# Tokens of a block ordered by column first, and attention's interior steps over 368 keys instead of 384

## The chip, the cores and the metric

The kernel runs on one core of one Trainium2 chip. Five engines work side by side there, each on its own queue of instructions: TensorE (PE; its weight loads are listed as PEld), VectorE (DVE), ScalarE (ACT), GpSimd (POOL) and SyncE (SP), which here issues nearly all transfers. Matmuls write to PSUM, a memory of eight banks of 128 x 512 fp32; everything else works in SBUF. The metric is the device time of one execution in microseconds; lower is better.

## The reference

One encoder layer over 1024 tokens that form a grid of 16 rows x 64 columns, with 1024 channels:

```python
u = rms_norm(x, g1); proj = u @ w_in            # q k v cB cC cH gA gB
q, k = rms_norm(q), rms_norm(k)                 # per head, 8 heads of 64
y_a = neighbourhood_attention(q, k, v, rpb) @ w_attn_branch
y_b = (cB * conv3(cC * cH)) @ w_conv_branch     # width 3 along the tokens
x = x + (sigmoid(gA) * y_a + sigmoid(gB) * y_b) @ w_o
x = x + square(relu(rms_norm(x, g2) @ w_mlp_in)) @ w_mlp_out
```

In the attention each token sees a window of 8 rows x 16 columns. The window is clamped inside the grid, and a learned bias by relative row and column is added to the scores before the softmax. The convolution runs over the tokens in their natural order, row after row.

## The kernel before

**Blocks.** The host cuts the grid into 8 blocks of 16 rows x 8 columns, so a block has 128 tokens, one for each partition of a tile. Within a block, token (r, c) stands at place 8r + c: rows first, and 8 neighbouring columns beside each other. All activations are kept in this block order. Only the convolution needs the natural order, because its taps are the token ahead and the token behind.

**Precision.** An fp32 value is kept as two fp16 halves, high and low, and a product takes three passes (`PASSES`: high x high, high x low, low x high).

**Attention** (lines 946 to 1033) runs in 64 steps: 4 pairs of heads `p`, 8 blocks `i` of queries, 2 heads `e` of the pair. A query block looks at the keys of its own block and of the two beside it. That makes 3 x 128 = 384 keys for the interior blocks 1 to 6 (48 steps) and 256 for the edge blocks 0 and 7 (16 steps). The stages of one step are spread over about 15 rounds of the loop at line 1044:

- `at_qk` (L959): two matmuls, for the two halves of q, into a PSUM bank of the tag "s", of which there are three.
- `at_max` (L973): one VectorE operation adds bias and mask to the negated scores, writes them to `sz` (five buffers), and takes the minimum, which frees the PSUM bank.
- `at_exp` (L982, ScalarE), `at_recip` (L986, L987, VectorE, once for a pair), `at_hi` (L995, ScalarE) and `at_lo` (L999, VectorE) give the probabilities as two fp16 halves in `P16`. One `P16` tile holds both heads of a pair, and three of them take turns.
- `at_turn` (L1004): SyncE issues one DMA transpose for a pair, `P16` to `PT`.
- `at_pv` (L1016): for every key block, pass and head one matmul with 64 columns of v as weights, 18 for an interior pair of steps. They are issued for four pairs together, in every eighth round.
- `at_out` (L1029, L1032): the result goes back into the place of q.

**Convolution.** The same rounds carry the matmuls of the gated convolution. `emit` (L1039) puts 7 to 9 of its matmuls behind each QK, from the generator `conv_mms`. For each of four channel groups j there are three projections g, two halves of 512 tokens each, 24 matmuls for a half. They use the three PSUM banks of the tag "d". `conv_post` takes a finished bank: for g = 0, ScalarE copies it into `z` (L847); for g = 1, VectorE multiplies it into `z` (L852); for g = 2, VectorE multiplies the convolved `cv` by it (L861). `z` and `cv` are in natural order (row, block, column), and the view `perm` walks them in block order. Between them, `conv_taps` makes the three taps (L868 ScalarE, L872 VectorE, L875 and L878 GpSimd). `conv_split` then scales the result and writes it to `BT` in two halves: L897 on ScalarE copies the high half, L902 on GpSimd subtracts for the low half. `BT` is read later by the matmuls of branch B.

**Order.** The order on each engine is the order in which the program issues the work: it is written out by hand in the loop at line 1044. Weights for later matmuls are prepared in the same rounds: `fill` advances generators of chunks (L266, L297, L306) as long as a running count of VectorE time, `debt`, stays under a bound. Tiles of the pool `p2` are opened when the tiles of the q/k stage are closed, and take over their memory; a first write to such memory waits for the last reader of what was there.

**Constants.** The bias of a query block against three key blocks comes from the host as `rel`, 128 x 768 for a pair of heads, and the masks as `masks`. Both are laid out in the order of the tokens within a block.

Of the kernel before, what the change touches and what calls it, by code (L numbers as in the profile page):

```python
# [11 lines left out]
F16 = mybir.dt.float16  # L12
BF16 = mybir.dt.bfloat16
I32 = mybir.dt.int32
AF = mybir.ActivationFunctionType
# [3 lines left out]
D = 1024  # L19
S = 1024  # L20
H = 8
HD = 64
# [30 lines left out]
def encoder_block(ctx: ExitStack, tc: tile.TileContext, x, weights, cols, gqk, rel, masks, out):  # L53
    nc = tc.nc
    V, A, G, T, SP = nc.vector, nc.scalar, nc.gpsimd, nc.tensor, nc.sync
# [10 lines left out]
    def bank(tag):  # L66
        return psum.tile([128, 512], F32, name="ps_" + tag, tag=tag, bufs=banks[tag])
# [80 lines left out]
    def spend(v=0, a=0):  # L148

        debt[0] += v  # L150
        debt[1] += a
# [44 lines left out]
    def ones_col():  # L196
        turn[0] = (turn[0] + 1) % 4
        return ones[:, 128 + turn[0]:129 + turn[0]]
# [192 lines left out]
    VT = base.tile([128, 8, 2, 512], F16, name="vT", tag="V")  # L391
# [207 lines left out]
    c = ones_col()  # L599
# [40 lines left out]
    c = ones_col()  # L640
# [128 lines left out]
    for n, (kind, b) in enumerate(todo):  # L769
# [3 lines left out]
        ps = bank("do"[n % 2])  # L773
# [5 lines left out]
        if n == 3:  # L779
# [52 lines left out]
    w2p = p2.enter_context(tc.tile_pool(name="p2", bufs=2, reuse_waits="tile"))  # L832

    def perm(t, half=None):
        v = t.rearrange("p (r b c) -> p b r c", r=16, b=8)
        return v if half is None else v[:, 4 * half:4 * half + 4]

    def conv_post(j, g, half, ps, d):

        ch = cConv[j]  # L840
        p3 = ps.rearrange("p (b r c) -> p b r c", b=4, r=16)
        if g == 0:
            if half == 0:
                d["z"] = w2p.tile([128, S + 2], F32, name="z", bufs=1)
                G.memset(d["z"][:, 0:1], 0.0)
                G.memset(d["z"][:, S + 1:S + 2], 0.0)
            A.activation(perm(d["z"][:, 1:S + 1], half), p3, AF.Copy, scale=sc[:, ch.inv])  # L847
            spend(0, 600)
            return
        if g == 1:  # L850
            zn = perm(d["z"][:, 1:S + 1], half)
            V.tensor_tensor(zn, p3, zn, op=OP.mult)  # L852
            spend(620)
            if half == 1:
                d["cv"] = w2p.tile([128, S], F32, name="cv", bufs=1)
                conv_tail.append(conv_taps(ch, d))
            return
        while not d.get("taps"):
            yield
        cv = d["cv"]  # L860
        V.tensor_tensor(perm(cv, half), p3, perm(cv, half), op=OP.mult)  # L861
        spend(620)
        if half == 1:
            conv_tail.append(conv_split(j, cv))

    def conv_taps(ch, d):
        z, cv, c = d["z"], d["cv"], ch.cwj
        A.activation(cv, z[:, 0:S], AF.Copy, scale=sc[:, at(c, 0)])  # L868
        spend(0, 1020)
        yield  # L870
        yield
        V.scalar_tensor_tensor(cv, z[:, 1:S + 1], sc[:, at(c, 1)], cv, op0=OP.mult, op1=OP.add)  # L872
        spend(1200)
        yield
        G.tensor_scalar(z[:, 2:], z[:, 2:], sc[:, at(c, 2)], 1.0, op0=OP.mult, op1=OP.mult)  # L875
        yield
        for c in range(0, S, 256):
            G.tensor_tensor(cv[:, c:c + 256], cv[:, c:c + 256], z[:, c + 2:c + 258], op=OP.add)  # L878
        yield
        yield  # L880
        d["taps"] = True

    def conv_split(j, cv):
        ch = cConv[j]
        m, s, inv = tmp(), tmp(), tmp()
        A.activation(BT[:, 1, j].bitcast(BF16), cv, AF.Square, accum_out=sc[:, m])
        spend(0, 1150)
        yield
        V.tensor_scalar(sc[:, m], sc[:, m], 1e-36, None, op0=OP.max)
        yield  # L890
        yield from pow2_half(m, 14, s, inv)
        mul(inv, ch.inv, at(rowsB, j))
        G.tensor_scalar(cv, cv, sc[:, s], 1.0, op0=OP.mult, op1=OP.mult)
        yield
        yield
        bh, bl = (BT[:, w, j].rearrange("p (b r c) -> p b r c", b=8, r=16) for w in range(2))
        A.activation(bh, perm(cv), AF.Copy)  # L897
        spend(0, 1020)
        yield
        pv = perm(cv)  # L900
        for b in range(0, 8, 2):
            G.tensor_tensor(bl[:, b:b + 2], pv[:, b:b + 2], bh[:, b:b + 2], op=OP.subtract)  # L902

# [41 lines left out]

    steps = [(p, i, e) for p in range(4) for i in range(8) for e in range(2)]
    N = len(steps)
    st, obank = {}, {}

    def rng(i):  # L950
# [3 lines left out]
    def at_qk(s):  # L954
        p, i, e = steps[s]
        lo, nb = rng(i)
        ps = bank("s")
        for w in range(2):
            T.matmul(ps[:, :nb * 128], QD[:, p, e, w, i * 128:(i + 1) * 128],  # L959
                     KD[:, 2 * p + e, lo * 128:(lo + nb) * 128], start=w == 0, stop=w == 1)  # L960
        st[s] = {"ps": ps, "n": nb * 128}

    def at_max(s):
        p, i, e = steps[s]
        d = st[s]
        t, m = bias[p]
        if 0 < i < 7:
            bm = m[:, e]
        else:
            bm = (t[:, e, 1:3] if i == 0 else t[:, e, 0:2]).rearrange("p b k -> p (b k)")  # L970
        z = d["z"] = w2p.tile([128, 384], F32, name="sz", bufs=5)
        d["mx"] = tmp()
        V.tensor_tensor_reduce(z[:, :d["n"]], d["ps"][:, :d["n"]], bm, sc[:, cneg], 3.0e38, OP.add, OP.min,  # L973
                               accum_out=sc[:, d["mx"]])
# [14 lines left out]

    def at_hi(s):  # L990
        d = st[s]
        n, e = d["n"], s % 2
        P = d["P"] = w2p.tile([128, 1536], F16, name="P16", bufs=3) if e == 0 else st[s - 1]["P"]
        d["hi"], d["lo"] = (P[:, (2 * e + w) * n:(2 * e + w + 1) * n] for w in range(2))
        A.activation(d["hi"], d["z"][:, :n], AF.Copy, scale=sc[:, d["r"]])  # L995

    def at_lo(s):
# [3 lines left out]
    def at_turn(s):  # L1001
        d = st[s]
        PT = d["PT"] = w2p.tile([128, 12, 128], F16, name="PT", bufs=6)
        SP.dma_start_transpose(PT[:, :4 * d["n"] // 128], d["P"][:, :4 * d["n"]])  # L1004

    def at_pv(s):
        p, i, _ = steps[s]
        lo, nb = rng(i)
        if i % 4 == 0:
            obank[p, i // 4] = bank("o")  # L1010
        O = obank[p, i // 4]
        seq = [(k, sp, sv) for k in range(nb) for sp, sv in PASSES]
        for n, (k, sp, sv) in enumerate(seq):
            for e in range(2):
                hd = (2 * p + e) * HD
                T.matmul(O[64 * e:64 * e + 64, (i % 4) * 128:(i % 4 + 1) * 128],  # L1016
                         VT[:, lo + k, sv, hd:hd + HD], st[s]["PT"][:, (2 * e + sp) * nb + k],
                         start=n == 0, stop=n == len(seq) - 1)
        for e in range(2):
            del st[s + e]  # L1020
# [20 lines left out]
    debt[:] = [0, 0]  # L1041
    for k in range(N + 16):
        p, w = k // 16, k % 16
        if p < 3 and w == 3:
            bias[p + 1] = bias_load(p + 1)
        if p < 3 and w in (12, 14):
            bias_make(*bias[p + 1], (w - 12) // 2)
            spend(550)
        ok = lambda d: 0 <= k - d < N
        debt[:] = [max(0, v - SPAN) for v in debt]  # L1050
# [44 lines left out]
    p3 = ExitStack()  # L1095
# [74 lines left out]

    def forms_split(ch, t, s, P):

# [91 lines left out]
    for n in range(8):  # L1264
# [3 lines left out]
        m = w3p.tile([128, 2, 512], F32, name="m", bufs=1)  # L1268
# [315 lines left out]
    y = []  # L1584
# [265 lines left out]
    for n in range(28):  # L1850
        s, o = n // 7, n % 7
        need(16 + n)
        P = OPS.pop(16 + n)
        inv = c2[s].inv
        for j in range(4):
            bk = anybank()
            for c, m in ((0, 256), (256, 256)) if n == 27 and j == 3 else ((0, 512),):
                ps = bk[:, c:c + m]
# [29 lines left out]

def _masks():

    r = np.arange(16)[:, None, None, None, None]
    c = np.arange(8)[None, :, None, None, None]
    bb = np.arange(3)[None, None, :, None, None]
    kr = np.arange(16)[None, None, None, :, None]
    kc = np.arange(8)[None, None, None, None, :]
    start = np.clip(r - 4, 0, 8)
    row = (kr >= start) & (kr < start + 8)
    rel = 8 * bb + kc - c
    colm = (rel >= 0) & (rel <= 15)
    full = (16, 8, 3, 16, 8)  # L1900
    row, colm = (np.broadcast_to(a, full).reshape(128, 384) for a in (row, colm))
    return np.stack([np.where(a, 0.0, NEG) for a in (row, colm)], 1).astype(mybir.dt.np(mybir.dt.bfloat16))

# [40 lines left out]
```

## Time and profile before

| | |
|---|---|
| time, median of 3 runs | 1207.05 us (1206.65 to 1208.08) |
| profiled execution, first to last instruction (its span) | 1205.3 us |
| granted TensorE clock, mean | 1.000 |
| QK matmuls, first and last start | 153.9 to 288.5 us |
| PV matmuls, first and last start | 187.6 to 304.8 us |

The profile shows one execution. The span leaves out what lies before its first and behind its last instruction, so it is a little shorter than a measured time. The page gives each engine's busy time, then the chain of waits that ended last. Its groups have the line, the engine, the operation, the tiles written and read, the shape and the count, then the busy time, the mean time of one instruction in ns, and the idle time of the engine just before them with what ended it. A view of one line gives minimum, median and maximum in ns with the first and last start. The timeline gives the start, the length, and in brackets the idle time ahead. An idle engine costs something only where TensorE, or whatever sets the end, waits for it.

### The profile page before, as it was taken

The numbers are of one execution on the slowest core, as the hardware profiler recorded it, in microseconds if no ns is written. First come the engines' busy times: TensorE is split into PE (matmuls) and PEld (weight loads), VectorE is DVE, ScalarE is ACT, GpSimd is POOL, SyncE is SP. The second block draws the span as 40 slices with busy tenths as digits, with TensorE's granted clock in tenths as the row PEclk, the third lists the DMA queues.
The fourth block names the chain that finished last, engine by engine and source line by source line (L and its number), as shares of the span: only waits on it lengthen the run. The fifth ranks groups of instructions, "written<-read, shape, count | busy, mean of one in ns | idle before, by whom it ended". The sixth has DMA issues, their size and how long they took to land.

```text
span 1205.3 us, 17076 instructions
## 1 busy us (share of the span) xinstructions
PE 1188.0 (99%) x6294; PEld 573.8 (48%) x6294; DVE 938.7 (78%) x1759; ACT 759.8 (63%) x1183; POOL 433.1 (36%) x280
## 2 busy tenths in 40 slices
PE   6999999999999999999999999999999999999998
PEld 4444445555444444444467444444444444444444
DVE  7777988988368787877878655545548999999997
ACT  7766679867554545337779778678676744746440
POOL 1640011222311112001004465565567471553662
PEclk9999999999999999999999999999999999999999
DMA  7766657676542211224386545445465925334202
GB/s 264 151 213 141 140 119 130 133 146 123 103 123 65 67 56 53 70 93 187 57 155 183 182 159 192 149 139 193 145 247 201 352 97 217 129 138 194 105 35 105
DMA packets 171012, 173.36 MB, mean 144 GB/s; under 512 B 131504, under 2 KB 132016, under 8 KB 166832
## 3 DMA queue, kind: packets, MB, share of 16 engines
q1 hardware_dynamic: 170352, 168.07, 47.9%
q10 hardware_dynamic: 576, 4.19, 0.8%
q8 instruction: 49, 0.80, 0.3%
q14 instruction: 35, 0.29, 0.1%
HBM read 102.51 MB, written 37.75 MB: 116 GB/s over the span
## 4 chain that ended last, share of the span: by engine, by line
PE 73%; DVE 9%; ACT 1%; issue 1%; DMA 1%; DVEq 0%; ACTq 0%
PE ps_d L210 26%; PE ps_s L210 23%; PE ps_o L210 16%; PE ps_d L1039 6%; DVE w_s L1163 2%; PE ps_o L1016 1%; PE ps_s L959 1%; DVE sg L1279 1%; DVE P L999 1%; DMA u2T<-v 1%; DVE sz L973 1%; ACT w_s L1167 0%; DVE sc L317 0%; DVE m L1281 0%; ACT sg L1245 0%
## 5 line engine op out<-in xcount | busy, mean ns | idle before, releaser
L210 PEld LDWEIGHTS <-ops 128*128 128x128 f16 x1356 | 132.4, 98 | 157.3
L210 PEld LDWEIGHTS <-w 128*128 128x128 f16 x1368 | 132.8, 98 | 140.0 <-DMA u2T<-v 0.6
L1039 PE MATMUL ps_d<-uT,w_ws 128*128 128x512 f16 x528 | 123.7, 379 | 0.1
L210 PE MATMUL ps_d<-ops 128*128 128x512 f16 (+1 forms) x528 | 118.3, 374 | 0.0
L1765 ACT ACTIVATE ops<-hf,sc 128x2048 f16<-128x2048 f32 x26 | 52.0, 2000 | 97.9 <-PE ps_o L210 35.2
L210 PE MATMUL ps_s<-ops 128*128 128x512 f16 x492 | 112.9, 379 | 0.0
L1152 POOL TENSOR_TENSOR tsum<-raw 128x512 f32<-128x512 f32 x28 | 46.0, 1658 | 149.6 <-ACT raw L1138 141.6
L1345 POOL TENSOR_TENSOR as<-as 128x512 f32<-128x512 f32 x56 | 77.5, 1384 | 39.3 <-ACT as L1625 36.0
L210 PEld LDWEIGHTS <-w_s 128*128 128x128 f16 x588 | 56.8, 98 | 69.4 <-DVE w_s L1163 1.9
L210 PE MATMUL ps_d<-u2x,w 128*128 128x512 f16 (+1 forms) x360 | 80.0, 372 | 0.0
L210 PEld LDWEIGHTS <-uT 128*128 128x128 f16 x504 | 49.0, 98 | 59.6 <-DMA uT<-u 0.8
L1039 PEld LDWEIGHTS <-w_ws 128*128 128x128 f16 x528 | 51.2, 98 | 54.5 <-DVE cv L861 0.4
L210 PE MATMUL ps_o<-ops 128*128 128x512 f16 x336 | 77.1, 379 | 0.0
L1767 DVE SCALAR_TENSOR_TENSOR ops<-hf,sc,ops 128x2048 f16<-128x2048 f32 x26 | 74.0, 2846 | 3.7 <-ACT ops L1765 3.7
L210 PE MATMUL ps_o<-u2T,w 128*128 128x512 f16 (+1 forms) x324 | 71.7, 371 | 0.0
L1138 ACT ACTIVATE raw<-raw,sc 128x256 f32<-128x256 f32 x172 | 71.0, 493 | 0.8 <-DMA raw<-in_weights 0.7
L1152 POOL TENSOR_TENSOR gsum<-raw 128x512 f32<-128x512 f32 x14 | 19.0, 1376 | 133.0 <-issue 72.8
L1167 ACT ACTIVATE w<-raw,sc 128x512 f16<-128x512 f32 (+1 forms) x28 | 24.6, 927 | 54.1 <-DVE sc L426 54.1
L297 DVE SCALAR_TENSOR_TENSOR w_ws<-raw,sc,w_ws 128x512 f16<-128x512 f32 (+2 forms) x72 | 51.2, 763 | 4.7 <-ACT w_ws L306 4.7
L1658 DVE TENSOR_TENSOR as<-ps_d,as 128x512 f32<-128x512 f32 (+1 forms) x14 | 9.4, 672 | 55.8 <-ACT as L1677 53.4
L210 PE MATMUL ps_s<-u2T,w 128*128 128x512 f16 (+1 forms) x252 | 52.7, 359 | 0.0
L982 ACT ACTIVATE sz<-sz,sc 128x384 f32<-128x384 f32 (+1 forms) x64 | 37.2, 582 | 22.5 <-DVE sc L973 15.0
(357 smaller groups left out, 2629.5 us busy)
## 6 DMA issues: line engine op xcount, KB each, us to landing
raw<-in_weights SPq DMA_DIRECT2D x88, 512.0 KB, 5.4
hs<-as SPq DMA_DIRECT2D x16, 1792.0 KB, 8.7
hf<-hs SPq DMA_DIRECT2D x26, 1024.0 KB, 6.3
w2x<-in_weights SPq DMA_DIRECT2D x16, 512.0 KB, 8.1
raw<-in_weights SPq DMA_DIRECT2D x16, 384.0 KB, 3.5
xt<-in_x SPq DMA_DIRECT2D x8, 512.0 KB, 10.0
gs<-s ACTq DMA_DIRECT2D x4, 1024.0 KB, 4.0
x<-in_x SPq DMA_DIRECT2D x8, 512.0 KB, 9.8
```

The lines of the kernel that those rows point to most:

```text
L210: T.matmul(ps, l, r, start=a, stop=b)
L297: V.scalar_tensor_tensor(lo, self.raw[p][:, o:o + m], sc[:, c:c + 1], hi, op0=OP.mult, op1=OP.subtract)
L959: T.matmul(ps[:, :nb * 128], QD[:, p, e, w, i * 128:(i + 1) * 128], KD[:, 2 * p + e, lo * 128:(lo + nb) * 128], start=w == 0, stop=w == 1)
L982: A.activation(z, z, AF.Exp, scale=-1.0, bias=sc[:, d["mx"]], accum_out=sc[:, d["sm"]])
L1039: T.matmul(ps, l, r, start=a, stop=b)
L1138: A.activation(v, v, AF.Copy, scale=sc[:, at(g, 4 * i + k)])
L1152: G.tensor_tensor(t[:, o], a, b, op=OP.add)
L1163: V.scalar_tensor_tensor(o(1), w, sc[:, s], o(0), op0=OP.mult, op1=OP.subtract)
L1167: A.activation(o(0), w, AF.Copy, scale=sc[:, s])
L1345: sub.tensor_tensor(z[o], z[a], z[b], op=op)
L1765: A.activation(P[:, 1, 0], hf, AF.Copy, scale=sc[:, Rs])
L1767: V.scalar_tensor_tensor(P[:, 1, 1], hf, sc[:, Rs], P[:, 1, 0], op0=OP.mult, op1=OP.subtract)
```

## The change

Within a block, token (r, c) now stands at place 16c + r: columns first, and the 16 rows of a column beside each other. A query in column c of its block needs, of the 24 columns of three key blocks, those from c to c + 15, so at most the columns 0 to 22. In the new order the unneeded column 23 is the last 16 of the 384 keys. The interior steps therefore compute scores, maximum, exponential and halves over 368 keys. In `P16` each part keeps its room of 384 with the last 16 columns set to zero once, by three memsets on GpSimd ahead of the loop; the transpose moves all of it as before, and for the third key block the PV matmuls contract over 112 rows. Three named tiles take the place of the rotating `P16`. The evacuations of the convolution read a PSUM bank whose 128 tokens of a block are now (column, row), walking it in the order of `z` and `cv`; L897 writes `BT` in the new order, and the four subtractions at L902 walk `cv` by rows. The host lays out input, output, bias and masks in the new order, outside the measured time.

```diff
     def conv_post(j, g, half, ps, d):
-        p3 = ps.rearrange("p (b r c) -> p b r c", b=4, r=16)
+        p3 = ps.rearrange("p (b c r) -> p b r c", b=4, r=16)
...
     def conv_split(j, cv):
-        bh, bl = (BT[:, w, j].rearrange("p (b r c) -> p b r c", b=8, r=16) for w in range(2))
-        A.activation(bh, perm(cv), AF.Copy)
+        A.activation(BT[:, 0, j].rearrange("p (b c r) -> p b r c", b=8, r=16), perm(cv), AF.Copy)
         spend(0, 1020)
         yield
-        pv = perm(cv)
+        bh, bl = (BT[:, w, j].rearrange("p (b c r) -> p b c r", b=8, r=16) for w in range(2))
+        pv = cv.rearrange("p (r b c) -> p b c r", r=16, b=8)
         for b in range(0, 8, 2):
             G.tensor_tensor(bl[:, b:b + 2], pv[:, b:b + 2], bh[:, b:b + 2], op=OP.subtract)
...
+    probs = [w2p.tile([128, 1536], F16, name=f"P16_{i}", bufs=1) for i in range(3)]
+    for t in probs:
+        G.memset(t.rearrange("p (q n) -> p q n", q=4)[:, :, 368:], 0.0)
...
     def at_qk(s):
-        ps = bank("s")
+        ps, n = bank("s"), 368 if nb == 3 else 256
         for w in range(2):
-            T.matmul(ps[:, :nb * 128], QD[:, p, e, w, i * 128:(i + 1) * 128],
-                     KD[:, 2 * p + e, lo * 128:(lo + nb) * 128], start=w == 0, stop=w == 1)
-        st[s] = {"ps": ps, "n": nb * 128}
+            T.matmul(ps[:, :n], QD[:, p, e, w, i * 128:(i + 1) * 128],
+                     KD[:, 2 * p + e, lo * 128:lo * 128 + n], start=w == 0, stop=w == 1)
+        st[s] = {"ps": ps, "n": n, "wide": nb * 128}
...
     def at_max(s):
-            bm = m[:, e]
+            bm = m[:, e, :368]
...
     def at_hi(s):
-        n, e = d["n"], s % 2
-        P = d["P"] = w2p.tile([128, 1536], F16, name="P16", bufs=3) if e == 0 else st[s - 1]["P"]
-        d["hi"], d["lo"] = (P[:, (2 * e + w) * n:(2 * e + w + 1) * n] for w in range(2))
+        n, e, m = d["n"], s % 2, d["wide"]
+        P = d["P"] = probs[s // 2 % 3]
+        d["hi"], d["lo"] = (P[:, (2 * e + w) * m:(2 * e + w) * m + n] for w in range(2))
...
     def at_turn(s):
-        SP.dma_start_transpose(PT[:, :4 * d["n"] // 128], d["P"][:, :4 * d["n"]])
+        SP.dma_start_transpose(PT[:, :4 * d["wide"] // 128], d["P"][:, :4 * d["wide"]])
...
     def at_pv(s):
+            r = 112 if k == 2 else 128
             for e in range(2):
                 hd = (2 * p + e) * HD
                 T.matmul(O[64 * e:64 * e + 64, (i % 4) * 128:(i % 4 + 1) * 128],
-                         VT[:, lo + k, sv, hd:hd + HD], st[s]["PT"][:, (2 * e + sp) * nb + k],
+                         VT[:r, lo + k, sv, hd:hd + HD], st[s]["PT"][:r, (2 * e + sp) * nb + k],
                          start=n == 0, stop=n == len(seq) - 1)
```

On the host, `x`, `rel`, `masks` and the output are permuted from (row, column) to (column, row) within a block.

More of the change, by code (lines that the diff above doesn't have):

```diff
@@ L1889, in _masks @@
 def _masks():
-    r = np.arange(16)[:, None, None, None, None]
-    c = np.arange(8)[None, :, None, None, None]
+    c = np.arange(8)[:, None, None, None, None]
+    r = np.arange(16)[None, :, None, None, None]
     bb = np.arange(3)[None, None, :, None, None]
-    kr = np.arange(16)[None, None, None, :, None]
-    kc = np.arange(8)[None, None, None, None, :]
+    kc = np.arange(8)[None, None, None, :, None]
+    kr = np.arange(16)[None, None, None, None, :]
     start = np.clip(r - 4, 0, 8)
@@ L1899, in _masks @@
     colm = (rel >= 0) & (rel <= 15)
-    full = (16, 8, 3, 16, 8)
+    full = (8, 16, 3, 8, 16)
     row, colm = (np.broadcast_to(a, full).reshape(128, 384) for a in (row, colm))
@@ L1913 @@
     x0 = a["x"][0]
-    arrays = {"x": x0.reshape(16, 8, 8, D).transpose(1, 0, 2, 3).reshape(S, D)}
+    arrays = {"x": x0.reshape(16, 8, 8, D).transpose(1, 2, 0, 3).reshape(S, D)}
     arrays["weights"] = np.concatenate([
@@ L1924 @@
     pad[:, 8:23] = np.asarray(rpb)[0]
-    rel = np.empty((4, 16, 8, 2, 3, 16, 8), np.float32)
+    rel = np.empty((4, 8, 16, 2, 3, 8, 16), np.float32)
     for r in range(16):
@@ L1929 @@
                 o = 8 * bb - c + 7
-                rel[:, r, c, :, bb] = pad[:, 15 - r:31 - r, o:o + 8].reshape(4, 2, 16, 8)
+                rel[:, c, r, :, bb] = pad[:, 15 - r:31 - r, o:o + 8].reshape(4, 2, 16, 8).transpose(0, 1, 3, 2)
     arrays["rel"] = rel.reshape(4, 128, 768)
@@ L1941 @@
     r = run_bass_kernel_spmd(nc, [arrays], core_ids=[0])
-    y = r.results[0]["out_y"].reshape(8, 16, 8, D).transpose(1, 0, 2, 3)
+    y = r.results[0]["out_y"].reshape(8, 8, 16, D).transpose(2, 0, 1, 3)
     return np.ascontiguousarray(y).reshape(1, S, D)
```

## The prediction, made before the result was known

> **What bounds the kernel now.** I read the page first, then the busy time of the stage that the change edits, its waits, and the timeline where TensorE waits.
>
> ```profile
> span 1205.3 us, 17076 instructions
> PE 1188.0 (99%) x6294; PEld 573.8 (48%) x6294; DVE 938.7 (78%) x1759; ACT 759.8 (63%) x1183; POOL 433.1 (36%) x280
> PE 73%; DVE 9%; ACT 1%; issue 1%; DMA 1%; DVEq 0%; ACTq 0%
> ```
>
> TensorE is busy for 99% of the span and carries 73% of the chain of waits: a column less on TensorE shortens the run, and work elsewhere costs only where TensorE comes to wait for it. The span is 1.75 us under the median of the runs (1207.05); I apply differences to that median.
>
> The change touches the attention stage alone, 150 to 305 us. Its busy times (sum over three windows of 155.00 us), and who waits there (us in total, times, longest):
>
> ```profile
> sum 155.00, PE 154.16 PEld 80.18 DVE 135.67 ACT 120.08 POOL 34.81; mean PE 51.38 PEld 26.73 DVE 45.22 ACT 40.03 POOL 11.60
> ```
>
> ```profile
> DVE w_ws L297 <- ACT w_ws L306: 3.1, 3, 1.8
> PEld L1016 <- issue: 2.4, 8, 0.4
> PE ps_s L959 <- DVE sc L973: 0.5, 1, 0.5
> PEld L1039 <- DVE cv L861: 0.4, 1, 0.4
> ```
>
> TensorE is full, but VectorE is at 135.67/155.00 = 88% and TensorE has already waited for it: VectorE stands right behind the bound. The timeline shows where, and which edited operations stand ahead:
>
> ```profile
> 157.93 1.35 ACT L847 ACTIVATE z<-ps_o,sc 128x512 f32<-128x512 f32 x2
> 160.76 1.15 DVE L297 SCALAR_TENSOR_TENSOR w_ws<-raw,sc,w_ws 128x384 f16<-128x384 f32 x2 [1.80 <-ACT w_ws L306]
> 162.64 0.69 DVE L852 TENSOR_TENSOR z<-ps_d,z 128x512 f32<-128x512 f32 x1
> 164.97 0.10 PEld L959 LDWEIGHTS <-qD 128*128 128x128 f16 x1 [0.34 <-issue]
> 169.83 0.68 DVE L852 TENSOR_TENSOR z<-ps_d,z 128x512 f32<-128x512 f32 x1
> 184.61 1.27 DVE L861 TENSOR_TENSOR cv<-ps_d,cv 128x512 f32<-128x512 f32 x2
> 185.34 1.63 PEld L1039 LDWEIGHTS <-w_ws 128*128 128x128 f16 x9 [0.40 <-DVE cv L861]
> 243.24 0.69 DVE L852 TENSOR_TENSOR z<-ps_d,z 128x512 f32<-128x512 f32 x1 [1.48 <-PE ps_d L1039]
> 251.71 0.69 DVE L852 TENSOR_TENSOR z<-ps_d,z 128x512 f32<-128x512 f32 x1
> 264.23 0.48 PE L959 MATMUL ps_s<-kD,qD 128*128 128x384 f16 x2 [0.48 <-DVE sc L973]
> 267.29 1.28 DVE L861 TENSOR_TENSOR cv<-ps_d,cv 128x512 f32<-128x512 f32 x2
> 285.77 0.68 DVE L852 TENSOR_TENSOR z<-ps_d,z 128x512 f32<-128x512 f32 x1
> 292.58 0.69 DVE L852 TENSOR_TENSOR z<-ps_d,z 128x512 f32<-128x512 f32 x1
> ```
>
> Scores have three PSUM banks, so the QK matmuls of step s wait until at_max (L973) of step s-3 has read its bank; conv groups have three too and wait for L852 and L861. There are **four contacts**: QK of step 6 at 164.97, a conv group at 185.34, QK of step 52 at 264.23, and the end of attention, where the last PV matmuls wait for the last transpose:
>
> ```profile
> L1004 SPq DMA_TRANSPOSE PT<-P x32: 1232/1432/2349, 168.4 to 299.3; - x32
> DMA to landing us min/median/max: 3.0/3.7/5.4
> L1016 PE MATMUL ps_o<-PT,vT x528: 216/219/243, 187.6 to 304.8; 128*64 128x128 f16 x176
> ```
>
> The last transpose is issued at 299.3 and lands 3.0 to 5.4 later, at 302.3 to 304.7; the last PV matmul starts at 304.8.
>
> **The change part by part.** *QK (L959).* The 48 interior steps issue two matmuls each over 368 columns instead of 384:
>
> ```profile
> 157.40 0.49 PE L959 MATMUL ps_s<-kD,qD 128*128 128x384 f16 x2
> 157.72 1.67 PE L1039 MATMUL ps_d<-uT,w_ws 128*128 128x512 f16 x7
> ```
>
> Two take 157.72 - 157.40 = 0.32 us, 0.42 ns a column: 96 x 16 x 0.42 ns = **0.64 us** less on TensorE. The edge steps keep 256.
>
> *Softmax (L973, L982, L995, L999).* Slope between the two widths:
>
> ```profile
> L973 DVE CUSTOM_DVE_ANT_0 sz<-ps_s,biasm,sc 128x384 f32<-128x384 f32 x48 | 29.4, 612 | 2.2 <-DVE sc L420 0.4 <-PE ps_s L959 0.2
> L973 DVE CUSTOM_DVE_ANT_0 sz<-ps_s,bias,sc 128x256 f32<-128x256 f32 x16 | 7.6, 479 | 0.7
> L982 ACT ACTIVATE sz<-sz,sc 128x384 f32<-128x384 f32 x48 | 29.3, 610 | 16.4 <-DVE sc L973 11.0 <-DVE sc L986 5.1
> L982 ACT ACTIVATE sz<-sz,sc 128x256 f32<-128x256 f32 x16 | 8.0, 499 | 6.0 <-DVE sc L973 4.0 <-DVE sc L986 2.0
> ```
>
> VectorE: (612 - 479)/128 = 1.04 ns an element, so 16 save 17 ns; L973 and L999 together 96 x 17 ns = 1.6 us. ScalarE: (610 - 499)/128 = 0.87 ns, and 96 x 14 ns = 1.3 us. They count only where a contact is fed, as below.
>
> *PV (L1016).* The third key block is contracted over 112 rows, not 128; still 18 matmuls of 128 columns per interior pair, and a matmul is paid by its columns (QK above). I take 0. A gain has no row to come from; the dear end is a rival.
>
> *Transposes (L1004).* Still all 1536 columns, pad included: same DMAs at the same place in SP's queue, nothing gained.
>
> *P16 tiles and memsets.* Three fixed tiles stand for three rotating ones, with the same distance of three pairs between a transpose and the next write. Three memsets of 64 elements go to the front of POOL's queue for the stage, ahead of the memsets of z, where POOL has waited 46.3 us for L750:
>
> ```profile
> L845 POOL MEMSET z<- 128x1 f32 x4 | 0.4, 99 | 46.4 <-DVE qs L750 46.3
> ```
>
> One of 64 elements lies between this 0.1 us and the 0.78 us of a 256-element L902 (below), so three take 0.3 to 0.6 us behind the same wait; behind them stand z's, whose first reader, L868, comes only when the second L852 (169.83) has completed z, 15 us later. 0; without that cover, up to 0.6 us.
>
> *Conv evacuation (L847, L852, L861).* Now the cost. PSUM holds a block as (column, row), while z and cv stay in (row, block, column) order. The PSUM operand, read straight through before, is now read with a step of 16 elements (64 bytes). No row of before has a single-element step, so I bound it:
>
> ```profile
> L847 ACT ACTIVATE z<-ps_d,sc 128x512 f32<-128x512 f32 x6 | 4.4, 733 | 0.0
> L736 ACT ACTIVATE qs<-ps_d,sc 128x512 f32<-128x512 f32 x8 | 5.4, 671 | 0.1
> L852 DVE TENSOR_TENSOR z<-ps_d,z 128x512 f32<-128x512 f32 x8 | 5.5, 687 | 1.8 <-PE ps_d L1039 1.8
> L1658 DVE TENSOR_TENSOR as<-ps_d,as 128x512 f32<-128x512 f32 x13 | 9.0, 692 | 55.8 <-ACT as L1677 53.4 <-PE ps_d L210 2.4
> ```
>
> The low end is 0: L852, whose z side runs in pieces of 8, takes 687 ns, and the unbroken L1658 takes 692. The high end comes from ScalarE: L847 writes z in 64 pieces and takes 733 against 671 for the unbroken L736, 62/64 = 1.0 ns a break. With a break at each of 512 elements, that is about 0.5 us: an estimate, and the same as one more element time each (512 x 1.04 = 0.53 us on VectorE, 512 x 0.87 = 0.45 on ScalarE). I take the high end, as the only row here in which breaks cost anything has that slope; both ends stay for the range.
>
> [...]
>
> *Sum over the contacts* at 0.53 us per VectorE and 0.45 per ScalarE evacuation. (1) L852 at 162.64 gives 0.53; the two L847 at 157.93 stand ahead of L306, for which VectorE had idled 1.80: 0.90. Together 1.43. (2) L852 at 169.83 and the first L861 at 184.61, 1.06, less some 20 shortened operations x 17 ns = 0.34: 0.72. (3) At 243.24 VectorE waits for TensorE, so earlier lateness is gone; L852 there and at 251.71 give 1.06, less 15 x 17 ns: 0.80. (4) Behind 264.23: two L861 and two L852, 2.12, less 0.36 for some 21 operations, and less what VectorE's own wait for ScalarE takes up at half its length:
>
> ```profile
> 294.20 0.17 DVE L986 RECIPROCAL sc<-sc 128x2 f32<-128x2 f32 x1 [0.94 <-ACT sz L982]
> ```
>
> 1.3. In all 1.43 + 0.72 + 0.80 + 1.3 = 4.25 us. At a contact TensorE takes VectorE's time, so its 0.64 vanishes in the waits; only what it saves away from them could show, and I leave it out. For the seven VectorE evacuations not named I add 0.2 only: from 185 to 243 no wait of TensorE on VectorE is listed, so there is slack. **+4.4 us: 1211.5**.
>
> *Conv split (L897, L902).*
>
> ```profile
> L897 ACT ACTIVATE bT<-cv 128x1024 f16<-128x1024 f32 x4 | 4.2, 1044 | 1.8 <-POOL cv L893 1.8
> L902 POOL TENSOR_TENSOR bT<-cv,bT 128x256 f16<-128x256 f32 x16 | 12.0, 782 | 15.9 <-ACT bT L897 15.9
> ```
>
> L897 now writes with a step; at 1.0 ns a break it would take 2.0 us instead of 1.04, four times, on an engine idle for 35 of 155 us. L902 reads cv at a step of 64 elements; the same end gives 16 x 0.26 us on POOL, busy 34.81 of 155. The first matmuls that read bT come 26 us behind the stage:
>
> ```profile
> 330.91 2.75 PE L210 MATMUL ps_d<-bT,w_wb 128*128 128x512 f16 x12
> ```
>
> 0; were that cover gone, 1.0 + 4 x 0.26 = 2 us, for the last conv block.
>
> **The rivals.** *No price for the step.* L852's row speaks for it, L847's against. Then TensorE keeps its 0.64, the contacts at 185.34 and at the end come earlier by the 0.34 of shortened work: -1.0, **1206.0**, not slower. It decides below about 0.1 us an evacuation. *Half price*, 0.27 and 0.22 us: the contacts come to 0.71, 0.20, 0.28 and 1.08 - 0.36 - 0.47 = 0.25, +1.4, **1208.5**; ScalarE's slope stands for a price, the zero of L852 against a full one. *TensorE changes shape for 112 rows.* Each entry into PV costs 0.3 us (2.4/8 idle on "issue"); twice in 24 interior pairs is 14 us: **1221**. Against it: the output half and its 64 columns stay. *It doesn't do what it says*: 16 columns come off the matmuls, but no DMA or PV matmul; if the interior scores were never on the path, +4.4 stays and the rival without a price ends at 1207.
>
> **How the numbers follow.** Full price 0.50, no price 0.28, half price 0.12, another array shape or more than the full price (POOL and VectorE colliding longer) 0.06, a gain beyond any sum here 0.04. A measurement tells about 0.2% (2.4 us) from no change. Slower by more: 0.50 + 0.06 + a sixth of the half-price case, 0.58; within: 0.38; faster: 0.04. The likeliest case's own range is 1209.2 (contacts 3 and 4 absorbed: 2.15 left) to 1213.5 (half of the seven unnamed evacuations counting too: 7 x 0.53/2 = 1.9); the whole range reaches down over the half price and the rival without a price, with the 0.34 idle at 164.97 gone as well: 1205.7 to 1213.5.
>
> **What would show it.** Right: L852 and L861 near 1.2 us, L847 near 1.2, L973 near 595 ns on 368 columns, longer waits of L959 for L973 and of L1039 for L861, and TensorE idle ahead of the last PV. Wrong: L852 and L861 still 0.69 (then 1206.0); idle "issue" time ahead of many more L1016; or longer evacuations with no new TensorE wait, which would mean that I took VectorE's slack for too small.

## The result, and the profile after

The changed kernel takes **1213.99 us** (median of 5 runs, 1212.6 to 1214.57) against 1207.29 us for the kernel before on the same chip: a ratio of 1.0055, 95% interval 1.0042 to 1.0067. It is slower by 6.7 us, where 4.4 were forecast; 1213.99 lies just above the range's end of 1213.5. The direction was right, but most of the time was not lost where the forecast had put it.

The page of the changed kernel (span, busy times, shares of the chain of waits):

```profile
span 1212.0 us, 17079 instructions
PE 1189.9 (98%) x6294; PEld 574.4 (47%) x6294; DVE 942.6 (78%) x1759; ACT 771.4 (64%) x1183; POOL 435.0 (36%) x283
PE 68%; DVE 8%; ACT 1%; DMA 1%; issue 1%; DVEq 0%; ACTq 0%
```

ScalarE has 771.4 us of work instead of 759.8, and TensorE's part of the chain falls from 73% to 68%. The groups of the stage, 150 to 330 us, show which instruction grew. After the bar stand the total in us and the mean in ns, then the idle time ahead and what ended it:

```profile
L896 ACT ACTIVATE bT<-cv 128x1024 f16<-128x1024 f32 x4 | 18.3, 4572 | 1.8 <-POOL cv L893 1.8
L902 POOL TENSOR_TENSOR bT<-cv,bT 128x256 f16<-128x256 f32 x16 | 14.3, 925 | 29.7 <-ACT bT L896 25.1 <-DMA qD<-gs 4.7
L852 DVE TENSOR_TENSOR z<-ps_d,z 128x512 f32<-128x512 f32 x8 | 5.5, 686 | 1.4 <-PE ps_d L1043 1.4
L861 DVE TENSOR_TENSOR cv<-ps_d,cv 128x512 f32<-128x512 f32 x8 | 5.1, 682 | 1.9 <-POOL cv L878 1.9
L847 ACT ACTIVATE z<-ps_d,sc 128x512 f32<-128x512 f32 x6 | 4.4, 732 | 0.0
L976 DVE CUSTOM_DVE_ANT_0 sz<-ps_s,biasm,sc 128x368 f32<-128x368 f32 x48 | 28.6, 596 | 2.0 <-DVE sc L420 0.4 <-PE ps_s L962 0.2
L985 ACT ACTIVATE sz<-sz,sc 128x368 f32<-128x368 f32 x48 | 28.6, 595 | 13.4 <-DVE sc L976 10.4 <-DVE sc L989 2.6
L962 PE MATMUL ps_s<-kD,qD 128*128 128x368 f16 x96 | 22.8, 319 | 1.1 <-DVE sc L976 1.0
L1020 PE MATMUL ps_o<-PT,vT 112*64 112x128 f16 x144 | 8.1, 219 | 0.0
```

The reader is to see two things. The evacuations that read PSUM at a step of 16 elements (L847, L852, L861) take 732, 686 and 682 ns; before, it was 733, 687 and 682. And the copy of the convolution's high half (L896, which was L897) takes 4572 ns instead of 1044. It reads `cv` in runs of 8 as before, but writes fp16 elements 16 places apart, in 32-byte steps.

The waits of the changed kernel in the same window (total, times, longest) show where TensorE came to stand still:

```profile
PE ps_s L962 <- DVE sc L976: 3.7, 4, 1.8
PE ps_o L1020 <- DMA PT<-P: 1.9, 1, 1.9
```

Before, it was 0.5 us in one QK wait, at 264.23. Of the four waits now the last is that of the same step, and no longer than it was. The new time stands in the other three: one of 1.75 us at 220.89, which the next timeline shows, and two here.

```profile
256.71 0.38 PE L962 MATMUL ps_s<-kD,qD 128*128 128x256 f16 x2 [0.93 <-DVE sc L976]
264.10 0.47 PE L962 MATMUL ps_s<-kD,qD 128*128 128x368 f16 x2 [0.52 <-DVE sc L976]
266.78 0.47 PE L962 MATMUL ps_s<-kD,qD 128*128 128x368 f16 x2 [0.48 <-DVE sc L976]
```

Neither kind of wait names ScalarE. The timeline of the changed kernel shows the way from ScalarE to TensorE (lines of several engines, others left out):

```profile
198.03 4.57 ACT L896 ACTIVATE bT<-cv 128x1024 f16<-128x1024 f32 x1
202.13 0.78 ACT L998 ACTIVATE P<-sz,sc 128x368 f16<-128x368 f32 x1
202.94 0.96 DVE L1002 SCALAR_TENSOR_TENSOR P<-sz,sc,P 128x368 f16<-128x368 f32 x1 [1.84 <-ACT P L998]
206.77 0.59 DVE L976 CUSTOM_DVE_ANT_0 sz<-ps_s,biasm,sc 128x368 f32<-128x368 f32 x1
...
220.89 0.38 PE L962 MATMUL ps_s<-kD,qD 128*128 128x256 f16 x2 [1.75 <-DVE sc L976]
```

From 198.03 nothing else runs on ScalarE until 202.13. The `at_hi` (L998) queued behind the copy is late, and so VectorE waits 1.84 us for it in `at_lo` (L1002); the `at_max` behind it (L976) starts at 206.77. VectorE is about 87% busy in the stage (134.76 of 155 us) and works off such a debt slowly: 18 us later the QK matmuls find their bank unread and wait 1.75 us.

The third copy, at 286.53, makes the end of attention late. The timeline of TensorE there, before and after:

```profile
302.85 2.17 PE L1016 MATMUL ps_o<-PT,vT 128*64 128x128 f16 x66
304.95 5.35 PE L210 MATMUL ps_s<-uT,w_ws 128*128 128x512 f16 x24
```

```profile
305.28 1.20 PE L1020 MATMUL ps_o<-PT,vT 128*64 128x128 f16 x36
308.35 1.36 PE L1020 MATMUL ps_o<-PT,vT 128*64 128x128 f16 x30 [1.87 <-DMA PT<-P]
309.63 7.04 PE L210 MATMUL ps_s<-uT,w_ws 128*128 128x512 f16 x24
```

The last PV matmuls wait 1.87 us for the last transpose. Then the first 24 matmuls behind the stage, of the same shape, take 7.04 us instead of 5.35. The windows of the changed kernel around them say why (length; busy time and count of PE, PEld, DVE, ACT, POOL; granted clock; DMA share; GB/s):

```profile
307.00:309.00 2.00, 0.65 (x18) 0.56 (x18) 1.29 (x2) 0.27 (x1) 0.31 (x1) 1.00 1.10 244
309.00:311.00 2.00, 1.86 (x18) 0.93 (x16) 0.92 (x8) 1.36 (x3) 0.01 (x1) 0.69 0.53 121
311.00:313.00 2.00, 2.00 (x7) 0.66 (x5) 0.67 (x2) 0.86 (x1) 1.11 (x1) 0.50 0.35 78
313.00:315.00 2.00, 2.00 (x10) 0.89 (x9) 0.00 (x0) 2.00 (x1) 0.00 (x0) 0.96 0.57 128
```

The granted clock fell to 0.50 behind the wait and came back some 3 us later. The PV matmuls, cut in two by their wait, also take 1.20 + 1.36 us instead of 2.17, 0.4 more, and the QK matmuls of the interior steps take 22.8 us instead of 23.5. So the loss adds up as (3.7 - 0.5) of QK waits + 1.9 of PV wait + 0.4 + (7.04 - 5.35 = 1.7) of clock - 0.7 = **6.5 us**, beside the 6.7 measured.

### The profile page after: what moved, and what is told of

It is laid out like the page before. It is cut to its first block, busy times and chain, and to the rows that moved or that the text cites. A ratio compares the mean times of both kernels' runs of the same rounds, so it can differ in the third digit from the quotient of the medians.

```text
span 1212.0 us, 17079 instructions
## 1 busy us (share of the span) xinstructions
PE 1189.9 (98%) x6294; PEld 574.4 (47%) x6294; DVE 942.6 (78%) x1759; ACT 771.4 (64%) x1183; POOL 435.0 (36%) x283
## 4 chain that ended last, share of the span: by engine, by line
PE 68%; DVE 8%; ACT 1%; DMA 1%; issue 1%; DVEq 0%; ACTq 0%
PE ps_d L210 26%; PE ps_s L210 23%; PE ps_o L210 16%; PE ps_d L1043 2%; DVE w_s L1167 2%; DVE sg L1283 1%; DMA u2T<-v 1%; ACT w_s L1171 0%; DMA PT<-P 0%; DVE P L1002 0%; DVE sc L317 0%; PE ps_o L1020 0%; DVE m L1285 0%; ACT sg L1249 0%; PE ps_s L962 0%
## 5 line engine op out<-in xcount | busy, mean ns | idle before, releaser
L306 ACT ACTIVATE w_ws<-raw,sc 128x512 f16<-128x512 f32 (+2 forms) x72 | 40.9, 636 | 13.2 <-DVE sc L279 13.2
```

What stands on the lines that cost most here:

```text
L306: A.activation(self.parts[:, 0, f + o:f + o + m], self.raw[p][:, o:o + m], AF.Copy, scale=sc[:, c:c + 1])
```

## The experiments

The theory that the runs were to test: L896's stepped write alone costs the time, because it holds ScalarE for 3.5 us more in one piece, and what is queued behind it starts later (at 202.13 in the timeline above). The rivals: the new order costs something in other places too; the total of ScalarE's work counts, not the hold; the part at the end of attention is only what the earlier copies left behind. All kernels but the probes compute the whole layer.

**The copy written straight.** The same values, in the new order; only the walk of the copy is turned about, so that it reads `cv` at a step of 64 elements and writes `BT` without a step.

```diff
-        A.activation(BT[:, 0, j].rearrange("p (b c r) -> p b r c", b=8, r=16), perm(cv), AF.Copy)
...
+        A.activation(bh, pv, AF.Copy)
```

> The changed kernel with one edit: L896 walks cv by rows (a step of 64 fp32) and writes BT straight, instead of reading runs of 8 and writing with a step of 16 fp16. Theory A (the four copies at L896, 4.57 us instead of 1.04, hold ScalarE's queue and are the whole loss): the copy takes 1.0 to 1.6 us and the time is 1205.5 to 1207, that is 0.3 to 1.8 us under before. Rival B (112-row weights, fixed P16 tiles, or the slower subtractions at L902 carry the loss): 1211 or more although the copy is short. If a read with a step costs ScalarE what the write does: the copy stays near 4.5 and the time near 1214.

Measured: 1207.11 us (11 runs) against 1207.4 before, ratio 1.0 (0.9991 to 1.0009). The copy's group and TensorE's waits in this kernel:

```profile
L898 ACT ACTIVATE bT<-cv 128x1024 f16<-128x1024 f32 x4 | 7.9, 1974 | 1.7 <-POOL cv L893 1.7
PE ps_s L962 <- DVE sc L976: 0.8, 2, 0.5
```

One instruction's write order carries the whole loss. Its read at a step of 256 bytes still costs 1974 instead of 1044 ns, above the 1.0 to 1.6 us expected, and that is covered: the time lies just above the expected range.

**The kernel before with a longer copy.** Nothing of the change is in it; the copy is done four times and a fifth time over five of eight blocks, all with before's walk.

```diff
-        A.activation(bh, perm(cv), AF.Copy)
+        for _ in range(4):
+            A.activation(bh, perm(cv), AF.Copy)
+        A.activation(bh[:, :5], perm(cv)[:, :5], AF.Copy)
```

> The kernel before with its copy at L897 done four times and a fifth time over 5 of 8 blocks, straight as before: some 4.4 us of ScalarE at each of the four places, no new token order and no narrowing. Theory A: 1213 to 1215.5, the loss of the changed kernel plus the 1.0 us that the narrowing no longer saves. Rival B: below 1209, as a longer copy alone is hidden.

Measured: 1216.23 us, ratio 1.0074 (1.0062 to 1.0087), a little more than expected. Its waits:

```profile
PE ps_s L961 <- DVE sc L975: 3.9, 4, 1.9
PE ps_o L1018 <- DMA PT<-P: 3.5, 2, 2.8
```

Without any new order, the same lateness gives nearly the same QK waits (3.9 beside 3.7), and a longer one ahead of the last PV. The five copies together take 4 x 1054 + 737 = 4953 ns, 0.4 us more than L896's 4572. The loss comes from the time for which ScalarE is held, whatever it is held with.

**The new order without the narrower steps.** As the kernel with straight writes, but with 384 keys, rotating `P16`, no memsets and 128 rows in PV.

```diff
-        ps, n = bank("s"), 368 if nb == 3 else 256
+        ps, n = bank("s"), nb * 128
...
-            r = 112 if k == 2 else 128
+            r = 128
```

> The straight write of the first run, and the narrowing undone: 384 keys, rotating P16 tiles, 128 rows, no memsets; only the token order is left. Theory A: the order costs nothing, within 0.5 us of before, and the first run is 0.6 to 1.2 us faster than this one (0.64 us of QK columns and some shorter waits). Rival B: this one is faster than the first run by 2 us or more.

Measured: 1207.46 us (11 runs), ratio 1.0003 (0.9994 to 1.0012). The order costs nothing that can be measured once the copy is written straight. The narrower steps are worth 0.35 us by the medians of these two kernels and 0.9 us by their spans (1205.5 and 1204.6). The intervals are about 1 us wide to each side, so this gain, expected at 0.6 to 1.2 us, isn't shown, though the QK group shows its term: 96 matmuls take 23.5 us here and 22.9 in the kernel with straight writes.

**Probes of stepped reads and writes.** A kernel of copies alone, which computes nothing of the layer and hands x through. Each form runs four times by itself.

```python
A.activation(o_rc, runs, AF.Copy)      # the changed kernel's copy
...
A.activation(o_cr, turned, AF.Copy)    # straight write, step on the read
...
A.activation(ws(2), straight, AF.Copy) # fp16 written at a step of 2, then 4, 8, 16
```

> No part of the layer is computed: x is copied to the output, and ScalarE, VectorE and GpSimd run the copy at L896 and the subtraction at L902 by themselves with different steps, four times each. Theory A1 (a write step of 32 bytes is what costs): ScalarE takes 1.0 us straight, 4.5 at a step of 16 fp16, and grows with the step, about 1.0 to 2.0 at a step of 2; reads with a step stay below 2.0. Rival A2 (the step on the write matters only together with runs of 8 on the read): the plain step of 16 takes 2 us or less. Rival A3 (any step costs, reads too): reads at a step of 16 fp32 take 3 us or more.

Measured: mean ns for 1024 elements read as fp32 from SBUF.

| engine | straight | fp16 write, step 2 | 4 | 8 | 16 | fp32 write, step 2 | 4 | 8 | 16 |
|---|---|---|---|---|---|---|---|---|---|
| ScalarE | 1056 | 1335 | 2471 | 4729 | 4482 | 1115 | 1998 | 2032 | 1917 |
| VectorE | 693 | 736 | | | 2357 | | | | 1042 |
| GpSimd (times 1.0, twice) | 1043 | | | | 4466 | | | | |

GpSimd's 4466 is with the changed kernel's walk. ScalarE's reads of fp32 at steps of 2, 4, 8 and 16, written straight, take 1107, 2001, 2034 and 1912 ns: not free, but far from the 3 us of rival A3. The plain step of 16, without runs on the read, takes 4482, so rival A2 falls too.

Three of the rows behind it, ScalarE with the changed kernel's walk, with the straight write of the first experiment, and VectorE at a step of 16:

```profile
L56 ACT ACTIVATE w<-cv 128x1024 f16<-128x1024 f32 x4 | 18.0, 4495 | 0.1
L58 ACT ACTIVATE w<-cv 128x1024 f16<-128x1024 f32 x4 | 7.7, 1922 | 0.1
L100 DVE CAST w<-cv 128x1024 f16<-128x1024 f32 x4 | 9.4, 2357 | 0.1
```

The changed kernel's copy by itself takes 4495 ns, so its 4572 in place is no collision with another engine. The step of the 2-byte write is the price: at a plain step of 16 it takes 4482 ns on ScalarE and 2357 on VectorE, beside 1056 and 693 straight, and with the changed kernel's walk 4466 on GpSimd, beside 1043. On ScalarE half the elements at a step of 16 take half (2342 ns). 4-byte elements written at the same step of elements take less than half as long, 1917 ns.

**Parts of the loss.** In the kernel with straight writes, the turned write is put back for one copy or two: the third alone, the first two, the last alone.

```diff
-        A.activation(bh, pv, AF.Copy)
+        if j in (2,):
+            A.activation(BT[:, 0, j].rearrange("p (b c r) -> p b r c", b=8, r=16), perm(cv), AF.Copy)
+        else:
+            A.activation(bh, pv, AF.Copy)
```

> As the kernel with straight writes, but the third copy alone (the one near 286 us) writes turned. Theory: the QK waits fall to those of the kernel with straight writes (below 1 us), while the last PV still waits about 1.9 us for its last transpose and the clock in 309 to 313 falls to about 0.6: 1.9 + 1.7 = +3.6 on 1207.1, so 1209.7 to 1211.7 us. Rival (the end of the stage is late by what the first two copies left behind, and the third comes too late to matter): 1206.5 to 1208 us, no wait of the last PV, clock above 0.95.

> As the kernel with straight writes, but the first two copies alone (near 198 and 241 us) write turned. Theory: QK waits about 3 to 4 us in four places, no wait of the last PV, and the clock after the stage stays above 0.95: +3 to +4 on 1207.1, so 1209.5 to 1211.5 us. Rival (QK waits are made up later, since the stage's end is set by VectorE's work in all): 1206.5 to 1208.5 us although the QK waits are there.

> As the kernel with straight writes, but the last copy alone (near 312 us, behind the stage, where ScalarE has idled for 7 us) writes turned. Theory: the 3.5 us more lie on an idle ScalarE and are covered, as the prediction had it for all four: within 0.1% of the kernel with straight writes, 1206.3 to 1208 us. Rival (evacuations of the next stage queue behind it and its low half on GpSimd is late for the matmuls that read it at 335): 1208.5 to 1211 us, with a new wait of TensorE between 313 and 340.

Measured against 1207.61 before: third copy 1210.92, ratio 1.0029 (1.0017 to 1.004); first two 1210.52, 1.0024 (1.0015 to 1.0033); last 1207.15, 0.9998 (0.9989 to 1.0007). Two lines of TensorE's waits with the third copy turned, then the one with the first two:

```profile
PE ps_o L1023 <- DMA PT<-P: 2.0, 1, 2.0
PE ps_s L965 <- DVE sc L979: 0.8, 2, 0.5
```

```profile
PE ps_s L965 <- DVE sc L979: 3.7, 4, 1.8
```

The parts come apart as the theory has it. The first two copies make the QK waits and leave the end of attention alone; the third makes the wait of the last PV and the drop of the clock (0.50 in the window 307 to 309), more than half of the loss. The last takes just as long (4553 ns) but runs at 306.9, behind the stage, and costs nothing that can be measured. Against each kernel's own run of before, and beside the kernel with straight writes (-0.29), they are worth 3.6, 3.2 and -0.2 us, together 6.6; all four in the changed kernel are worth 7.0.

**The turned copy cut in four.** Four instructions of two blocks each, with attention going on between them.

```diff
-        A.activation(BT[:, 0, j].rearrange("p (b c r) -> p b r c", b=8, r=16), perm(cv), AF.Copy)
-        spend(0, 1020)
-        yield
...
+        bt, pt = BT[:, 0, j].rearrange("p (b c r) -> p b r c", b=8, r=16), perm(cv)
+        for b in range(0, 8, 2):
+            A.activation(bt[:, b:b + 2], pt[:, b:b + 2], AF.Copy)
+            spend(0, 255)
+            yield
```

> The changed kernel, with each of its four turned copies cut into four instructions of two blocks each, between which the attention steps go on. ScalarE does the same work (about 4 x 4.6 = 18 us in all; 1.15 to 1.2 us each), but is held no longer than 1.2 us at a time, which is about what before's copy held it. Theory (the uncut hold of an in-order queue is what reaches TensorE): nearly all of the 6.7 us goes; 1207 to 1209 us, QK waits at most 1 us, no wait of the last PV above 0.5 us, clock above 0.95 at 309 to 313. Rival (the 14 us more of ScalarE's time in the stage, or the stepped writes themselves, cost the time whatever the pieces): 1212 to 1215 us, waits as in the changed kernel.

Measured: 1217.77 us, ratio 1.0086 (1.0073 to 1.0098): slower still, against the theory's 1207 to 1209. But its trace names another wait:

```profile
PE ps_d L1045 <- DVE cv L861: 4.4, 2, 4.2
PE ps_o L1022 <- DMA PT<-P: 2.1, 2, 1.5
PE ps_s L964 <- DVE sc L978: 1.3, 2, 1.0
```

```profile
260.32 1.15 ACT L868 ACTIVATE cv<-z,sc 128x1024 f32<-128x1024 f32 x1 [2.02 <-POOL bT L904]
```

The QK waits did shrink, from 3.7 to 1.3 us; the waits for the last transposes didn't (2.1 us). But the three extra turns moved the subtraction on GpSimd (now L904) three rounds back. It is the last reader of the one `cv` buffer, so the next group's first write to `cv` (L868) stood 2.02 us at the head of ScalarE's queue, and the convolution's evacuations came late for their banks. As a test of pieces against total the run is lost; it shows a second place where this plan has no slack. The next two kernels ask the question without moving anything.

**As much ScalarE work, spread out.** The kernel with straight writes, with five extra copies of 512 elements for each channel group, one in each of five turns of the convolution's taps; the group's own copy writes over them later. The first two are shown.

```diff
         yield
+        A.activation(BT[:, 0, j, 0:512], KD[:, 0, 0:512], AF.Copy)
         V.scalar_tensor_tensor(cv, z[:, 1:S + 1], sc[:, at(c, 1)], cv, op0=OP.mult, op1=OP.add)
         spend(1200)
         yield
+        A.activation(BT[:, 0, j, 0:512], KD[:, 0, 0:512], AF.Copy)
...
```

> The kernel with straight writes, and for each conv block five extra straight ScalarE copies of 512 elements (kD to bT, written over later by the copy of the block), one in each of five different turns of the conv work, with the order of all else kept. They add some 5 x 0.55 = 2.7 us a block, so that ScalarE has about as much to do in the stage as in the changed kernel, but is never held for more than 2 us. Theory (the hold at one place counts, not the total): the loss against the kernel with straight writes is at most 1.5 us: 1206.8 to 1208.6 us, QK waits at most 1.5 us, no wait of the last PV above 0.5. Rival (the total counts): 1211 to 1214.5 us with waits as in the changed kernel.

**The turned copy cut in two**, in the turns that the copy and the subtraction have already.

```diff
-        A.activation(BT[:, 0, j].rearrange("p (b c r) -> p b r c", b=8, r=16), perm(cv), AF.Copy)
-        spend(0, 1020)
+        bt, pt = BT[:, 0, j].rearrange("p (b c r) -> p b r c", b=8, r=16), perm(cv)
...
+        A.activation(bt[:, 0:4], pt[:, 0:4], AF.Copy)
+        spend(0, 1020)
+        yield
+        A.activation(bt[:, 4:8], pt[:, 4:8], AF.Copy)
```

> The changed kernel with each turned copy cut into two halves in the two neighbouring turns that the copy and the subtraction already have, so that nothing else is moved (the cut in four had moved the subtraction three turns back). Each half holds ScalarE about 2.35 us. Theory: the lateness is that of 2.35 - 1.04 = 1.3 us twice with other work between: QK waits 1 to 2.5 us, the last PV waits at most 1.2 us; 1208 to 1211.5 us. Rival (total): 1212.5 to 1215 us, waits as in the changed kernel.

Measured against 1207.38 before: spread out 1206.62 (11 runs), ratio 0.9995 (0.9986 to 1.0003); cut in two 1211.06, ratio 1.0036 (1.0023 to 1.005). The busy times of the stage, 150 to 305, in three kernels: the changed one, the one with the extra work spread out, and the one cut in two.

```profile
sum 155.00, PE 151.06 PEld 77.93 DVE 134.76 ACT 127.20 POOL 34.41; mean PE 50.35 PEld 25.98 DVE 44.92 ACT 42.40 POOL 11.47
```

```profile
sum 155.00, PE 153.98 PEld 80.36 DVE 135.55 ACT 131.84 POOL 36.06; mean PE 51.33 PEld 26.79 DVE 45.18 ACT 43.95 POOL 12.02
```

```profile
sum 155.00, PE 152.53 PEld 79.06 DVE 133.09 ACT 126.94 POOL 35.11; mean PE 50.84 PEld 26.35 DVE 44.36 ACT 42.31 POOL 11.70
```

With the extra work spread out ScalarE is busier in the stage, 131.84 us, than in the changed kernel, 127.20, and nothing measurable is lost (the time is even a little below the range expected); its one QK wait is the 0.5 us of the kernel before. So the total of ScalarE's time over the stage is not the cause. For the end of attention alone this run can't tell: of its extra copies only one, of 0.61 us at 294.89, stands between the third group's copy and the last `at_hi`. Cut in two, with holds of about 2.4 us, the time lies between:

```profile
PE ps_s L964 <- DVE sc L978: 2.1, 3, 1.1
PE ps_o L1022 <- DMA PT<-P: 2.0, 2, 1.8
```

Its QK waits are as expected, while the wait ahead of the last PV, 2.0 us, is above the 1.2 that the theory allowed: two halves delay the last transposes as much as one whole. ScalarE's timeline tells why, from the third group's copy to the last three `at_hi`, in the kernel before, in the changed one and in the one cut in two (lines between are left out):

```profile
288.27 0.61 ACT L982 ACTIVATE sz<-sz,sc 128x384 f32<-128x384 f32 x1 [0.89 <-DVE sc L973]
295.12 1.40 ACT L995 ACTIVATE P<-sz,sc 128x384 f16<-128x384 f32 x3
```

```profile
286.53 4.57 ACT L896 ACTIVATE bT<-cv 128x1024 f16<-128x1024 f32 x1
299.77 1.38 ACT L998 ACTIVATE P<-sz,sc 128x368 f16<-128x368 f32 x3
```

```profile
285.10 2.40 ACT L899 ACTIVATE bT<-cv 128x512 f16<-128x512 f32 x1
298.25 1.40 ACT L1000 ACTIVATE P<-sz,sc 128x368 f16<-128x368 f32 x3
```

In the kernel before, where the copy starts at 284.25, this stretch takes 12.3 us and has one idle gap of 0.89 us. The kernel with straight writes has filled that gap (its copy is 0.93 us longer) and takes 12.3 us as well. In the changed kernel and in the one cut in two ScalarE is busy without a gap, and the stretch takes 14.6 us in both (286.53 to 301.15, 285.10 to 299.65). So at the end of attention it is the sum of ScalarE's work beyond the gap that makes the last transposes late, in one piece or in two; the length of a piece shows at the first two copies, where the QK waits fell from 3.7 to 2.1. The clock stayed at 1.00 in this run: 1.6 us less of QK waits and no 1.7 of clock account for the 3 us by which it is quicker than the changed kernel.

None of these kernels is faster than the one before by more than the measurement tells: those with straight writes, with the order alone and with the work spread out all have 1.0 within their intervals.

## Why the prediction was right in sign and wrong in place

- **What bounds the kernel**: right. TensorE sets the time and VectorE stands close behind; but for the clock's 1.7 us, what was lost shows as waits of TensorE, through VectorE or the transposes. Of the four contacts only the last PV was hit. QK of step 6 and the convolution group at 185 lie ahead of the first long copy, and the QK wait near 264 kept its 0.48 us. The largest QK wait, 1.75 us at 220.89, stands between 185 and 243, where the prediction had read slack from the absence of listed waits; the slack there was less than the lateness that the copy brought.
- **QK, softmax, PV, transposes, memsets**: right. QK gained 0.7 us (its 96 matmuls went from 23.5 to 22.8), L976 went from 612 to 596 ns and L985 from 610 to 595. The PV matmuls over 112 rows take 219 ns, those over 128 take 220, and in the kernel with straight writes the idle time on "issue" ahead of them is that of before, 2.4 us in 8 times. The memsets take 152 ns each, behind the wait for L750 that was named as their cover.
- **The evacuations**: the step that carried the forecast's 4.4 us, and it failed. "I take the high end", 0.53 and 0.45 us for each, and the sum over four contacts, 4.25 us, rest on it. The price measured 0 in all three groups (732 ns beside 733, 686 beside 687, 682 beside 682), so the low end, drawn from L852's 687 beside L1658's 692, was the right one. The slope of 1.0 ns a break came from L847's *writes* to `z`, not from a read of PSUM: a row of the wrong kind was carried over. (Whether breaks are what L847's 62 ns were paid for, no run tells.)
- **The conv split**: the other failed step. The term put at 0 is where the loss lay, 6.6 us by the parts, and it has two faults. "At 1.0 ns a break it would take 2.0 us": it took 4.57, 4.5 ns an element written. And "an engine idle for 35 of 155 us" was taken as cover. That average held for work in small pieces spread over the stage (131.84 us of work cost nothing). One piece of 4.57 us delays what stands behind it in the queue, and that was `at_hi` and `at_exp`, on which VectorE and the transposes wait; and ahead of the last transposes the idle time was 0.89 us, not a share of 35. The prediction's own sums had the chain from ScalarE to VectorE (the 1.80 and 0.94 us waits) but didn't follow it from this line. It asked only who reads `BT`.
- L897 is the one write with a step in the diff. The probes show the price of such a write at 32 bytes (4482 ns beside 1056 straight) and below that as well: fp16 at a step of 4 bytes takes 1335 ns, at 8 bytes 2471.
- **L902**: 925 instead of the 1.04 us estimated, from 782; covered, as costed.
- **The rival "no price for the step"** is what the kernel with straight writes realises. It gave -1.0 us; -0.3 was measured (1207.11 beside 1207.4), which can't be told from either -1.0 or 0.
- That +4.4 lay near the 6.7, and on the right side of 0, is luck: a price that wasn't there stood in for one that wasn't seen. Two terms were in no part of the working: the drop of the clock, 1.7 us, and the first two copies' QK waits, 3.2. (The upper end of the range, 1211.5 + 1.9, is 1213.4 rather than 1213.5; the measured time lies above both.)

## What to carry to other kernels

Before an access pattern is moved from one side of an instruction to the other, look at which side has 2-byte elements: here the copy with the step on the fp32 read takes 1.9 times the straight one (1974 ns beside 1044) and that with the step on the fp16 write 4.4 times (4572). And when an instruction on an engine with idle time grows, ask how long it holds that engine in one piece, what stands behind it in the queue, and how much idle time that queue has left before the next deadline: the idle share of a whole stage said nothing of the last 12 us, where 0.89 us was left.

## What was not expected of the hardware

**Writes of 2-byte elements with a step.** ScalarE went from 1056 to 1335, 2471 and 4729 ns at steps of 4, 8 and 16 bytes, then stayed (4482 at 32). fp32 writes go to 1998 ns at 16 bytes and stay there (2032 at 32, 1917 at 64). VectorE at 32 bytes takes 3.4 times its straight copy (2357 to 693), GpSimd 4.3 times (4466 to 1043).

**The clock behind a wait.** The granted clock fell to 0.50 behind, or at the end of, waits of 1.87, 2.04, 2.83 and 4.17 us, and in the kernel cut in four after 1.50 and 0.62 us with 18 PV matmuls between, but not after 1.75 and 1.81, and not after 1.91 at the QK of the kernel before with a longer copy:

```profile
221.73 0.38 PE L961 MATMUL ps_s<-kD,qD 128*128 128x256 f16 x2 [1.91 <-DVE sc L975]
```

```profile
221.00:223.00 2.00, 1.27 (x7) 0.68 (x7) 1.85 (x5) 1.22 (x3) 1.78 (x2) 1.00 0.83 260
```

So the length of the wait alone doesn't decide. How long the low clock lasts follows from the shares of the 2 us windows: in the changed kernel, where they show 0.69, 0.50 and 0.96, a clock of 0.50 for part of the first and last window gives 0.31 x 2/0.5 + 2 + 0.04 x 2/0.5 = 3.4 us. Worked out in the same way it is 3.4 us in the kernel with the third copy turned, in the kernel before with a longer copy and behind the 1.50 and 0.62, and 6.8 us, twice as long, behind the 4.17. What else decides, and why the low clock lasts that long, no run here shows: the wait of 1.87 us, behind which the clock fell, and that of 1.81, behind which it did not, both have 36 PV matmuls ahead of them and more behind.
